# Three edits to the first third of a hybrid encoder layer: rotary tables after the first norm, gate stores on ScalarE's queue, half of the memory's values inside the scans

## The chip, the cores and the metric

The kernel runs on one core of one Trainium2 chip. The core has five engines, each working through its own list of instructions in order: TensorE (PE) for matrix products, VectorE (DVE) and ScalarE (ACT) for elementwise work, GpSimd (POOL) for some elementwise work, and SyncE (SP), which here only starts transfers (DMAs). An engine that reaches an instruction whose input is not there stands until it is, and everything behind that instruction in its list stands with it. The metric is the device time of one execution in microseconds (us), lower is better.

## The reference, cut to what matters

One layer works on x (1024 tokens x 1024) and on a memory of 256 tokens:

```
h    = rms_norm(x) ; proj = h @ w_in            # q,k,v of attention, q,k,v of DeltaNet, gate, alpha, beta
attn = window_attention(rope(q), rope(k), v)    # 8 heads, 2 kv heads, +-128 tokens
dn   = gated_delta(conv(q,k,v), decay, beta)    # 4 heads, two directions, then * silu(gate)
x    = x + rms_norm([attn, dn] @ w_out)
x    = x + rms_norm(cross_attention(rms_norm(x), rms_norm(mem), w_cq, w_ckv, w_co))
out  = x + rms_norm(swiglu(rms_norm(x)))
```

Three pieces of this matter here. `rope` needs the sine and cosine of position x frequency for 1024 tokens (the rotary tables). The gate is silu(h @ w_gate), 512 columns, and is multiplied onto the DeltaNet's output. The cross-attention needs keys and values of the memory, mem @ w_ckv, each 256 x 1024. All products are taken in three parts of reduced-precision pieces (high x high, high x low, low x high), so each weight tile is cast (`whi`, on ACT) and its remainder taken (`wlo`, on DVE or POOL) before PE may use it.

## The kernel before

Stage 1 (about 0 to 200 us of the span) loads x in eight tiles of 128 tokens. Each tile is squared and summed (ACT, L230), its root inverted (ACT L168, DVE L169), scaled (DVE, L233, tile `xt`), transposed on PE (L239), and cast into a high part (ACT, L241, `hhi`) and a low part (DVE, L242, `hlo`). Two halves of four tiles each make `hT`. Then come the projections of the DeltaNet's q, k and v (PE, L276, weights by `load_w`, L103 to L125). Each projection is followed by a convolution: ACT copies it into `cp` (L298), DVE adds four shifted products (L301, `acc`, four instructions of 128x1024), ACT takes the silu (L302). `decays` (L486 to L493), `key_products`, `query_products` and `base_inverse` (L558 and L560: sixty small dependent DVE instructions for each pair of heads) follow in the order of `ORDER_1`.

The rotary tables (L398 to L415) belong to stage 1 in the text, behind the products for alpha and beta. For each half of the tokens, DVE issues eight instructions on `ang` (L405 to L411, with three of L410) and two on `sct` (L414, L415), and ACT two sines (L412, L413). They read `posi`, which a DMA on SP's queue loads (L400). The tables are first read in stage 2, by `attn_proj`.

Stage 2 (about 200 to 372 us) runs `ORDER_2`: A are the projections of the attention's q and k with the rotation, V its values, G the four gate projections, L the four `levels` that finish the inverses, W two attention windows each. `gate_proj` takes two banks of PSUM, writes silu of each into `gt` (ACT, L814), and stores it in `d_gate` in DRAM by a DMA on SP's queue (L815). `gt` shares the buffers "rop" (two) with the attention projections.

Stage 3 (about 372 to 520 us) runs `ORDER_3`: M is the memory's norm, each `s01` one step of the two groups' scans over the eight chunks (the ninth flushes), W two windows, K one of eight blocks of the memory's keys (24 products of 128x256 on PE, remainder on POOL), V one of two halves of its values (48 products of 128x512, in four weight chunks of 512 KB, remainder on DVE, L104). A tail of windows and values, until about 559 us, leads to the first product with `w_out` (`mid_gemm`, L1102, tile `pmg`). The weights `wraw`, `whi` and `wlo` are rings of two buffers each, used by everything that calls `load_w`, and PSUM is one pool of five banks (`pc`) in stage 3, which must be empty before `mid_gemm` gets its banks.

What sets the order on each engine is a list scheduler that runs when the kernel is built: it places instructions by its own model of time, by order in the text, and by `high_priority` for weight loads; `tc.issue_after(x)` adds that an instruction comes behind x. So a change of three lines can move any instruction of these stages. Within the first `mid_gemm` the lists of before and after come together again.

The semaphores that DMAs count on are eight, DMAHW0 to DMAHW7, taken in turn by all DMAs of the schedule; a DMA waits until the DMA eight places ahead of it, which had the same one, is done.

Of the kernel before, what the change touches and what calls it, by code (L numbers as in the profile page):

```python
# [19 lines left out]
P = 128  # L20
# [4 lines left out]
HALF = 512  # L25
# [10 lines left out]

ORDER_1 = ("k0 k1 E0 K0 U0 E1 K1 U1 S0 q0 v0 q1 C0 v1 E2 C1 k2 E3 k3 q2 K2 U2 v2 K3 U3 S1 q3 C2 v3 C3 B0 B1").split()
ORDER_2 = "L0 L1 A4 V A0 A1 G0 G1 L2 L3 W W W A2 A3 G2 G3 W".split()
ORDER_3 = ("M " + "s01 W K " * 5 + "s01 K " * 3 + "s01 V V").split()


_NAMES = ["ident", "mUi", "mLi", "m5", "m6", "band0", "band1", "band2", "mU", "mL", "ones"]
# [34 lines left out]
def tile_hybrid_block(  # L77
# [6 lines left out]
    nc = tc.nc  # L84
    x, mem, out = x[0], mem[0], out[0]
    w_in, w_out, w_cq, w_ckv, w_co = w_in[0], w_out[0], w_cq[0], w_ckv[0], w_co[0]
# [7 lines left out]
    def f32(ap):  # L94
        return ap.bitcast(F32)
# [4 lines left out]
    def split(hi, lo, src, scale=None, eng=None):  # L100

        if scale is None:
            nc.scalar.copy(hi, src)  # L103
            return (eng or nc.vector).tensor_tensor(lo, src, f32(hi), ALU.subtract)  # L104
        nc.scalar.activation(hi, src, AF.Identity, scale=scale)
        return nc.vector.scalar_tensor_tensor(lo, src, scale, f32(hi), ALU.mult, ALU.subtract)
# [68 lines left out]
    def gain(n, k):  # L175
        return cols[:, gain_at[n] + k:gain_at[n] + k + 1]
# [7 lines left out]
    d_gate = dram.tile([512, S], F32, name="d_gate")  # L184
# [38 lines left out]
    for hf in range(2):  # L223
# [12 lines left out]
        for k in range(KT):  # L236
# [5 lines left out]
            cut = nc.vector.scalar_tensor_tensor(lo[:, k, :], pt, g, f32(hi[:, k, :]), ALU.mult, ALU.subtract)  # L242
# [36 lines left out]
    def proj(src_cols, eng=None):  # L279
        whi, wlo = load_w(src_cols, KT, P, eng)  # L280
        pp = [pg.tile([P, 512], F32, tag="pg", name="pg") for _ in range(2)]
        gemm_b(whi, wlo, hT, pp)
        return pp
# [36 lines left out]
    t1 = pa1.enter_context(pool("t1b", 1, side="right"))  # L320

    wab = t1.tile([P, KT, 16], F32, tag="wab", name="wab", bufs=1)
    nc.sync.dma_start(wab, w_in[:, 2816:2832].rearrange("(k p) n -> p k n", p=P))
    wabr = tb.tile([P, KT, P], F32R, tag="V", name="wabr", bufs=1)
    with tc.issue_after(scaled.ins):
        nc.vector.tensor_scalar(wabr, hT[0][0].bitcast(F32)[:, :, 0:P], 0.0, None, ALU.mult)
# [70 lines left out]
    sct = ra.tile([P, 2, S], F32, tag="sct", name="sct")  # L397
    sinT, cosT = sct[:, 0], sct[:, 1]  # L398
    posi = wt.tile([P, S], I32, tag="inv1", name="posi")
    nc.sync.dma_start(posi, positions[0].partition_broadcast(P))  # L400
    for hf in range(2):
        sl = slice(hf * HALF, (hf + 1) * HALF)
        work = wt.tile([P, 2, HALF], F32, tag="inv0", name="ang")
        ang, rn = work[:, 0], work[:, 1]
        nc.vector.tensor_copy(ang, posi[:, sl])  # L405
        nc.vector.tensor_scalar(ang, ang, rope_f, None, ALU.mult)
        nc.vector.tensor_scalar(rn, ang, 1.0 / (2.0 * math.pi), MAGIC, ALU.mult, ALU.add)
        nc.vector.tensor_scalar(rn, rn, MAGIC, None, ALU.subtract)
        for cc in (c1, c2, c3):
            nc.vector.scalar_tensor_tensor(ang, rn, -cc, ang, ALU.mult, ALU.add)  # L410
        nc.vector.tensor_scalar(ang, ang, math.pi, -math.pi, ALU.min, ALU.max)  # L411
        nc.scalar.activation(sinT[:, sl], ang, AF.Sin, scale=rope_s)  # L412
        nc.scalar.activation(cosT[:, sl], ang, AF.Sin, scale=0.5)  # L413
        nc.vector.tensor_tensor(cosT[:, sl], cosT[:, sl], cosT[:, sl], ALU.mult)  # L414
        nc.vector.tensor_scalar(cosT[:, sl], cosT[:, sl], -2.0, 1.0, ALU.mult, ALU.add)  # L415
# [342 lines left out]
    def issue(order, table):  # L758
        for o in order:
            table[o[0]](*(int(c) for c in o[1:]))  # L760
# [48 lines left out]
    def gate_proj(h):  # L809

        pp = proj(w_in[:, 2304 + h * P:2304 + (h + 1) * P])
        for hf in range(2):
            gt = trp.tile([P, HALF], F32, tag="rop", name="gt")
            nc.scalar.activation(gt, pp[hf], AF.Silu)  # L814
            nc.sync.dma_start(d_gate[h * P:(h + 1) * P, hf * HALF:(hf + 1) * HALF], gt)  # L815

    issue(ORDER_2, {"A": attn_proj, "V": value_proj, "G": gate_proj, "L": levels, "W": next_windows})
    dump("d_q", d_q); dump("d_k", d_k); dump("d_gate", d_gate)
    p1.close()
# [186 lines left out]
    def scan_step(pairs):  # L1006

        for _ in range(4):
            for s_ in pairs:
                next(s_, None)  # L1010

    issue(ORDER_3, {"s": lambda *gs: scan_step([scans[g] for g in gs]), "W": next_windows, "M": memory_norm,
                    "K": next_keys, "V": next_values})
# [452 lines left out]
    for k in range(KT):  # L1466
        pt = turned_k(first_rows, k, (PG, PN, PX, PG)[k // 2])
        cut = split(x1h[:, k, :], x1l[:, k, :], pt, gain("ffn", k))
# [406 lines left out]
```

## Time and profile before

| what | value |
|---|---|
| median of 3 runs | 1534.7 us (1529.84 to 1535.23) |
| the profiled execution | 1540.26 us, span 1538.0 us |
| mean granted clock of TensorE | 0.989 |
| PE busy | 1481.9 us (96% of the span) |
| DVE busy | 1095.6 us (71%) |
| ACT busy | 787.4 us (51%) |
| POOL busy | 364.7 us (24%) |

The profile is of one execution. "Busy" is the time in which an engine executes; the rest is idle, and the profile names what ended each idle stretch (the releaser). PEclk is the share of TensorE's full clock that was granted in a stretch: at 0.5 a product takes twice as long, and PE is busy for it all the same, so a stage loses time in two ways, by PE's idle time and by a low clock. A row of the timeline reads: start in us, duration, engine, line, operation, output<-inputs, shapes, count, and in brackets the idle time before it and what ended that. SPq is the queue on which SP starts DMAs.

### The profile page before, as it was taken

The page shows a single profiled execution, that of the slowest core. Times are in us where ns is not written, and L with a number is a line of the kernel's source. Part 1 is how long each engine was busy: PE and PEld are TensorE (multiplying, and loading weights), DVE is VectorE, ACT ScalarE, POOL GpSimd, SP SyncE. Part 2 cuts the span into 40 slices and gives each one's busy share as a digit, 9 for nine tenths or more (in the row PEclk, how much of TensorE's full clock was granted, in tenths as well). Part 3 has the DMA queues.
Part 4 walks back from the last instruction along what each step waited for, and adds up shares of the span by engine and source line. Part 5 has one row for each costly group of instructions (what it writes and reads, how often), then busy time and mean ns, then how long its engine had stood idle before and what let it go on. Part 6 is the DMA issues. An engine that isn't in the chain of part 4 may idle for free.

```text
span 1538.0 us, 21325 instructions
## 1 busy us (share of the span) xinstructions
PE 1481.9 (96%) x7437; PEld 1245.3 (81%) x7437; DVE 1095.6 (71%) x1801; ACT 787.4 (51%) x1608; POOL 364.7 (24%) x394
## 2 busy tenths in 40 slices
PE   6999999998899989999999999999999999999998
PEld 5888888787899768888788867888888888888787
DVE  6768998366798856447657768776868774696566
ACT  7578844567548755455545685323232232454533
POOL 0011133331237202152300101433434332000020
PEclk9999999999999989999999999999999999999999
DMA  6235464455998655357733743433435333853355
GB/s 200 68 103 152 118 187 136 143 171 141 318 306 253 223 187 194 111 195 255 248 121 134 229 165 118 129 123 124 132 108 171 124 99 108 311 210 101 110 176 166
DMA packets 257751, 256.34 MB, mean 167 GB/s; under 512 B 18128, under 2 KB 190317, under 8 KB 257645
## 3 DMA queue, kind: packets, MB, share of 16 engines
q1 hardware_dynamic: 257645, 255.00, 51.8%
q8 instruction: 58, 0.95, 0.3%
q14 instruction: 48, 0.39, 0.1%
HBM read 178.63 MB, written 73.70 MB: 164 GB/s over the span
## 4 chain that ended last, share of the span: by engine, by line
PE 70%; DVE 10%; DMA 8%; ACT 6%; issue 4%; SPq 2%; POOL 0%; DVEq 0%; ACTq 0%; POOLq 0%
PE pg L276 9%; PE pE L1512 8%; PE pD L1512 8%; PE pA L1512 6%; PE pmg L1102 6%; PE pdX L1718 5%; PE pst L1318 5%; PE pB L1512 4%; PE pcq L276 3%; PE pdA L1718 2%; PE psc L841 2%; PE pdD L1718 2%; DMA wpart<-in_w_co_dram 1%; DMA b<-in_w_down_dram 1%; PE pco L1217 1%
## 5 line engine op out<-in xcount | busy, mean ns | idle before, releaser
L103 ACT CAST whi<-wraw 128x1024 fp32r<-128x1024 f32 x96 | 100.9, 1052 | 131.4 <-DMA wraw<-in_w_gate_up_dram 35.7
L276 PE MATMUL pg<-hlo,whi 128*128 128x512 f32 x352 | 141.3, 401 | 0.0
L276 PE MATMUL pg<-hhi,whi 128*128 128x512 f32 x352 | 140.9, 401 | 0.1
L276 PE MATMUL pg<-hhi,wlo 128*128 128x512 f32 x352 | 140.5, 399 | 0.0
L104 POOL TENSOR_TENSOR wlo<-wraw,whi 128x1024 fp32r<-128x1024 f32 x36 | 87.4, 2429 | 179.3 <-ACT whi L103 179.3
L1512 PE MATMUL pA<-b,whi 128*128 128x512 f32 x352 | 110.7, 396 | 3.6 <-ACT m L1539 2.8
L104 DVE TENSOR_TENSOR wlo<-wraw,whi 128x1024 fp32r<-128x1024 f32 x60 | 73.2, 1221 | 49.7 <-ACT whi L103 41.6
L1512 PEld LDWEIGHTS pA<-b,whi 128*128 128x128 f32 x352 | 65.7, 189 | 19.0 <-ACT m L1539 4.0
L276 PEld LDWEIGHTS pg<-hhi,whi 128*128 128x128 f32 x352 | 67.4, 191 | 14.0 <-ACT hhi L241 0.7
L276 PEld LDWEIGHTS pg<-hlo,whi 128*128 128x128 f32 x352 | 67.3, 191 | 13.0
L276 PEld LDWEIGHTS pg<-hhi,wlo 128*128 128x128 f32 x352 | 67.5, 192 | 12.7
L1718 PE MATMUL pdX<-dhl,whi 128*128 128x512 f32 x264 | 76.1, 390 | 1.7 <-DVE zv L1777 0.8
L1595 POOL TENSOR_TENSOR act<-act,up 128x512 f32<-128x512 f32 x33 | 50.8, 1538 | 83.2 <-DVE up L1594 61.8
L103 ACT CAST whi<-araw 128x1024 fp32r<-128x1024 f32 (+1 forms) x36 | 35.3, 981 | 68.4 <-PE pdX L1718 27.6
L1512 PE MATMUL pA<-b,wlo 128*128 128x512 f32 x176 | 69.4, 395 | 0.5 <-DVE wlo L104 0.5
L104 DVE TENSOR_TENSOR wlo<-araw,whi 128x1024 fp32r<-128x1024 f32 (+1 forms) x36 | 40.8, 1133 | 36.8 <-ACT whi L103 36.7
L1567 POOL TENSOR_TENSOR sr<-wraw 128x512 f32<-128x512 f32 x22 | 30.7, 1397 | 151.4 <-DMA wraw<-in_w_gate_up_dram 102.1
L301 DVE SCALAR_TENSOR_TENSOR acc<-cp,cols,acc 128x1024 f32<-128x1024 f32 x48 | 61.9, 1298 | 0.2
L1718 PEld LDWEIGHTS pdX<-dhl,whi 128*128 128x128 f32 x264 | 49.3, 188 | 13.0 <-issue 1.1
L103 ACT CAST dhl<-b 128x512 fp32r<-128x512 f32 x66 | 40.3, 620 | 31.0 <-PE pdA L1718 13.2
L1512 PE MATMUL pB<-s0h,s1h 128*128 128x512 f32 x176 | 54.7, 392 | 1.2 <-ACT s1h L103 1.2
L103 ACT CAST s0h<-sr 128x512 fp32r<-128x512 f32 x22 | 13.7, 622 | 80.7 <-POOL sr L1567 80.2
(503 smaller groups left out, 4314.4 us busy)
## 6 DMA issues: line engine op xcount, KB each, us to landing
wraw<-in_w_gate_up_dram SPq DMA_DIRECT2D x54, 512.0 KB, 3.8
kv<-d_kv SPq DMA_DIRECT2D x32, 512.0 KB, 7.0
wraw<-in_w_in_dram SPq DMA_DIRECT2D x22, 512.0 KB, 3.7
b<-in_w_down_dram SPq DMA_DIRECT2D x20, 512.0 KB, 6.6
araw<-d_as SPq DMA_DIRECT2D x20, 512.0 KB, 3.7
pz<-d_pz SPq DMA_DIRECT2D x32, 256.0 KB, 7.1
wraw<-in_w_ckv_dram SPq DMA_DIRECT2D x16, 512.0 KB, 6.7
wraw<-in_w_out_dram SPq DMA_DIRECT2D x16, 512.0 KB, 3.8
```

The costliest lines, as they stand in the source:

```text
L103: nc.scalar.copy(hi, src)
L104: return (eng or nc.vector).tensor_tensor(lo, src, f32(hi), ALU.subtract)
L276: nc.tensor.matmul(p_, w[:, k, :], ah[a][:, k, :], start=(k == 0 and i == 0), stop=(k == nk - 1 and i == 2))
L301: nc.vector.scalar_tensor_tensor(acc, cp[:, t:t + S], taps[t], acc, ALU.mult, ALU.add)
L841: nc.tensor.matmul(out[:, d, h, :], lt[:, d, h, :], rt[:, d, h, :], start=True, stop=True)
L1102: nc.tensor.matmul(pp[t], act[a][:, k, tt], w_[:, kk, :], start=(k == 0 and i == 0), stop=(k == KT - 1 and i == 2))
L1217: nc.tensor.matmul(po, vr_[a][:, kt, cs], pts[kt][b_], start=(kt == 0 and i == 0), stop=(kt == 1 and i == 2))
L1318: nc.tensor.matmul(bank, a[:, tt], w, start=(start and i == 0), stop=(stop and i == 2), skip_group_check=not check)
L1512: nc.tensor.matmul(out_, w[a][:, k, :], xx[b_][:, k, :], start=(start and k == 0 and i == 0), stop=(k == HK - 1 and i == 2), skip_group_ch ...
L1567: nc.gpsimd.tensor_tensor(s[0], b_[:, 0:HK], b_[:, HK:], ALU.add)
L1595: nc.gpsimd.tensor_tensor(o_, o_, up, ALU.mult)
L1718: nc.tensor.matmul(banks[t], a[:, k - k0, tt], w, start=(first and k == 0 and i == 0), stop=(k == NB - 1 and i == 2), skip_group_check=not ...
```

## The change

Rotary tables: the DMA of `posi` is placed behind that of `wab` (the weights of alpha and beta) on SP's queue, and the first instruction on `ang` of each half behind `cut`, the last `hlo` of the first norm. Gate stores: the same eight DMAs are started by ScalarE. Values: `ORDER_3` had its fifth to eighth key blocks in a row and both V at the end; now one V stands behind the sixth scan step, and the last K behind the ninth.

```diff
-ORDER_3 = ("M " + "s01 W K " * 5 + "s01 K " * 3 + "s01 V V").split()
+ORDER_3 = ("M " + "s01 W K " * 5 + "s01 V " + "s01 K " * 2 + "s01 K V").split()
...
-    nc.sync.dma_start(wab, w_in[:, 2816:2832].rearrange("(k p) n -> p k n", p=P))
+    wab_load = nc.sync.dma_start(wab, w_in[:, 2816:2832].rearrange("(k p) n -> p k n", p=P))
...
-    nc.sync.dma_start(posi, positions[0].partition_broadcast(P))
+    with tc.issue_after(wab_load.ins):
+        nc.sync.dma_start(posi, positions[0].partition_broadcast(P))
...
-        nc.vector.tensor_copy(ang, posi[:, sl])
+        with tc.issue_after(cut.ins):
+            nc.vector.tensor_copy(ang, posi[:, sl])
...
-            nc.sync.dma_start(d_gate[h * P:(h + 1) * P, hf * HALF:(hf + 1) * HALF], gt)
+            nc.scalar.dma_start(d_gate[h * P:(h + 1) * P, hf * HALF:(hf + 1) * HALF], gt)
```

The changed file has two lines more from L401 on, so L814 before is L816 after, and so on (L405 is L407, L301 stays).

The first place is VectorE's list while the second half of x is normed. Before:

```order
L405 CAST ang<-posi 128x512
L169 RECIPROCAL rs<-rs 128x1
L406 TENSOR_SCALAR ang<-ang,CE 128x512
L233 TENSOR_SCALAR xt<-xt,rs 128x1024
L169 RECIPROCAL rs<-rs 128x1
L269 TENSOR_SCALAR nega<-nega 128x8
L407 TENSOR_SCALAR ang<-ang 128x512
L233 TENSOR_SCALAR xt<-xt,rs 128x1024
```

After, at the same place and on to the first convolution:

```order
L169 RECIPROCAL rs<-rs 128x1
L233 TENSOR_SCALAR xt<-xt,rs 128x1024
L169 RECIPROCAL rs<-rs 128x1
L269 TENSOR_SCALAR nega<-nega 128x8
L233 TENSOR_SCALAR xt<-xt,rs 128x1024
L261 CAST mU_r<-CE 128x128
L262 CAST mL_r<-CE 128x128
L326 TENSOR_SCALAR wabr<-hhi_152 128x1024
L242 SCALAR_TENSOR_TENSOR hlo_239<-ps,gcol,hhi_238 128x512 x8
L327 CAST wabr<-wab 128x8x16
L328 TENSOR_TENSOR wabr<-wab,wabr 128x8x16
L407 CAST ang<-posi 128x512
```

No instruction on `ang` stands ahead of the last two `xt` and the eight `hlo` any more; the twenty instructions of the tables stand between those of the first convolutions and of alpha and beta.

The second place is ScalarE's list at the end of stage 2, with the waits that each instruction carries. Before:

```order
L692 ACTIVATE sc,ssum<-sc,nm 128x384 x3
L814 ACT_TABLE_LOAD [waits DMAHW3_49]
L814 ACTIVATE gt<-pg 128x512 [waits PE_49]
L696 ACT_TABLE_LOAD
L696 ACTIVATE es<-es 128x4 [waits Pool_49]
L956 ACTIVATE mjk,mss<-mt 128x1024
L956 ACTIVATE mjk,mss<-mt 128x1024 [waits DMAHW5_49,Activation_49]
L103 CAST ph<-ptw 128x512 [waits PE_49]
L103 CAST ph<-ptw 128x512 [waits DVE_49,PE_49]
L814 ACT_TABLE_LOAD [waits DMAHW4_49]
L814 ACTIVATE gt<-pg 128x512 [waits PE_49]
```

After:

```order
L816 ACT_TABLE_LOAD [waits DMAHW2_49]
L816 ACTIVATE gt<-pg 128x512 [waits PE_49]
L817 DMA d_gate<-gt 128x512 [waits DMAHW5_49,Activation_49]
L958 ACTIVATE mjk,mss<-mt 128x1024
L958 ACTIVATE mjk,mss<-mt 128x1024 [waits Activation_49]
L103 CAST ph<-ptw 128x512 [waits DVE_49,PE_49]
L816 ACTIVATE gt<-pg 128x512 [waits DMAHW4_49,PE_49]
L817 DMA d_gate<-gt 128x512 [waits DMAHW7_49,Activation_49]
```

Two loads of activation tables are gone there (over the whole list 34 stand where 36 stood: L814's four became three, and L696's four became three), and the two stores now stand in ScalarE's list, each with a wait on a DMA semaphore. Six of the eight stores carry such a wait.

The third place is PE's list where the first half of the values begins. Before, it begins behind the last transposes of the scans' flush (L933, `psc<-ident,ol`):

```order
L709 MATMUL ptw<-ident,sc 128x128 x4
L714 MATMUL pow<-ph,vhl 128x512
L933 MATMUL psc<-ident,ol 128x128 x4
L997 MATMUL pcv<-whi,mT_4077 128x512
L997 MATMUL pcv<-whi,mT_4078 128x512
L997 MATMUL pcv<-wlo,mT_4077 128x512
```

After, it begins between steps of the scans (L843, `psc`, are the scans' products), some 230 products earlier in the list, and 24 key products (`pck`) and the second half follow the flush:

```order
L685 MATMUL psw<-khi,qs 128x384
L685 MATMUL psw<-klo,qs 128x384
L935 MATMUL psc<-ident,ol 128x128 x4
L999 MATMUL pcv<-whi,mT_4077 128x512
L999 MATMUL pcv<-whi,mT_4078 128x512
L999 MATMUL pcv<-wlo,mT_4077 128x512
```

So 48 of the 96 value products left the stretch between the flush and the first `pmg`, and 24 key products came to it. The number of instructions on PE, DVE and POOL is unchanged; ScalarE has eight DMAs more and two table loads fewer, SP eight DMAs fewer.

## The prediction

> **What bounds the kernel now.** I read the page first, then PE by stage, then what each idle stretch of PE waited for.
>
> ```profile
> span 1538.0 us, 21325 instructions
> ...
> PE 1481.9 (96%) x7437; PEld 1245.3 (81%) x7437; DVE 1095.6 (71%) x1801; ACT 787.4 (51%) x1608; POOL 364.7 (24%) x394
> ...
> PE 70%; DVE 10%; DMA 8%; ACT 6%; issue 4%; SPq 2%; POOL 0%; DVEq 0%; ACTq 0%; POOLq 0%
> ```
>
> PE is busy for 96% and makes 70% of the chain that ended last. The change takes no product away, so it can only win PE's idle time, 1538.0 - 1481.9 = 56 us, and what a low clock adds. It moves instructions in the first 560 us alone; there the stages read (columns: length, then busy time and count of PE, PEld, DVE, ACT, POOL, then PE's clock):
>
> ```profile
> 24.00:50.00 26.00, 22.16 (x101) 17.75 (x100) 18.16 (x39) 13.59 (x22) 0.00 (x0) 0.87 0.21 56
> 50.00:130.00 80.00, 80.00 (x403) 66.88 (x402) 60.78 (x80) 57.95 (x136) 8.29 (x22) 1.00 0.40 112
> 130.00:250.00 120.00, 117.22 (x623) 99.36 (x622) 110.18 (x201) 78.18 (x210) 25.31 (x50) 1.00 0.48 138
> 340.00:376.00 36.00, 32.42 (x181) 27.29 (x180) 18.18 (x47) 27.43 (x55) 8.05 (x16) 0.95 0.43 133
> 376.00:420.00 44.00, 39.30 (x294) 35.53 (x293) 34.66 (x93) 25.46 (x59) 9.23 (x8) 1.00 1.04 319
> 420.00:519.00 99.00, 94.84 (x759) 90.92 (x758) 88.77 (x236) 69.70 (x203) 52.47 (x62) 1.00 0.78 240
> 519.00:560.00 41.00, 34.43 (x153) 27.66 (x152) 27.67 (x57) 24.79 (x47) 2.17 (x2) 0.91 0.82 276
> ```
>
> Three stretches are open: the first norm (24 to 50), the end of stage 2 (340 to 376), and the tail behind the scans (519 to 560). From 50 to 130 PE never stops; from 130 to 250 DVE is at 110.18 / 120 = 92%, and in the scans at 88.77 / 99 = 90%, so there PE and DVE are near their limit together.
>
> **Term 1, the rotary tables.** In the first norm the chain is posi, ang, xt, transposes, hlo, products:
>
> ```profile
> 19.75 0.43 SPq L400 DMA_DIRECT2D posi<-in_positions_dram  x1
> 23.24 0.29 ACT L168 ACTIVATE rs<-ss,mhalf 128x1 f32<-128x1 f32 x1
> 27.19 0.43 DVE L405 CAST ang<-posi 128x512 f32<-128x512 int32 x1 [4.66 <-DMA posi<-in_positions_dram]
> 29.19 0.75 DVE L233 TENSOR_SCALAR xt<-xt,rs 128x1024 f32<-128x1024 f32 x1
> 31.18 2.14 DVE L410 SCALAR_TENSOR_TENSOR ang<-ang 128x512 f32<-128x512 f32 x3
> 34.49 1.11 PE L239 MATMUL ps<-ident,xt 128*128 128x128 f32 x4 [2.79 <-DVE hlo L242]
> ...
> 49.65 7.25 PE pg L334 x32
> ...
> 24.00:34.50 10.50, 6.66 (x39) 4.88 (x37) 7.17 (x18) 5.66 (x10) 0.00 (x0) 0.96 0.53 139
> 34.50:41.00 6.50, 6.50 (x23) 5.45 (x24) 5.92 (x11) 3.93 (x6) 0.00 (x0) 0.54 0.00 0
> ```
>
> The root that the last `xt` needs was there at 23.5 (second row), but DVE stood 4.66 us before `ang` for a transfer that has nothing to do with it, and scaled that `xt` only at 29.19. More `ang` work (2.14 us) stands ahead of `hlo`, PE runs dry for 2.79 us, and its clock falls to 0.54 for the 6.5 us that follow. Idle 10.50 - 6.66 = 3.8 us, slow clock 6.5 x 0.46 = 3.0 us: 6.8 us. After, nothing of the tables stands ahead of `xt` and `hlo`, so I take all 6.8 as won by the time the first projections end; the next limit is `hlo` itself, eight instructions that ACT feeds one by one.
>
> [...]
>
> The cost is that the tables' work is still to do:
>
> ```profile
> 24.00:50.00 26.00, 8.49 (x16) 2.48 (x4) 0.87 0.21 56
> 24.00:50.00 26.00, 2.22 (x4) 2.48 (x4) 0.87 0.21 56
> L301 DVE SCALAR_TENSOR_TENSOR acc<-cp,cols,acc 128x1024 f32<-128x1024 f32 x48 | 61.9, 1298 | 0.2
> ```
>
> The same window asked for `ang` alone (first row) and `sct` alone (second) gives DVE 8.49 + 2.22 = 10.7 us and ACT 2.48 us; the table load before the sines is merely at another place. All twenty DVE instructions now stand between the taps of the first convolutions (1298 ns each), ahead of the alpha and beta chain and of `decays`. DVE has 80 - 60.78 = 19.2 us idle from 50 to 130, so 10.7 us fit, but not all of that idle time can be moved into: DVE waits there for ACT and PE too. Ends: all 6.8 us kept; or DVE's list is the path and 10.7 - 6.8 = 3.9 us are lost. I take 4.5 won, nearer the upper end, because PE in that row is 80.00 of 80 on other projections; 2.3 us go where DVE runs at 92% (130 to 250). The moved `posi` DMA passes two weight loads and `wab`; those start 0.4 us earlier, and `ang` wants it ten us later than before: nothing.
>
> **Term 2, the gate stores.**
>
> ```profile
> SPq L815 <- ACT gt L814: 10.4, 4, 6.2
> SPq L815 <- ACT bs L632: 8.7, 2, 8.3
> L815 SPq DMA_DIRECT2D d_gate<-gt x8: 320/330/552, 270.7 to 372.6; - x8
> DMA to landing us min/median/max: 2.0/3.3/6.9
> PE ptm L966 <- ACT gt L814: 0.3, 1, 0.3
> ...
> 364.06 1.28 ACT L814 ACT_TABLE_LOAD   x1
> 365.97 1.28 ACT L696 ACT_TABLE_LOAD   x1
> 370.21 0.50 PE L714 MATMUL pow<-ph,vhl 128*128 128x512 f32 x1 [2.71 <-ACT ph L103]
> ...
> 373.00 0.87 SPq L856 DMA_DIRECT2D kv<-d_kv  x2
> ```
>
> SP stood 10.4 + 8.7 = 19.1 us before these stores. Queued behind them are `qr`, `pz`, `kv` and the key weights. No wait of PE from 40 to 376 names any of them, so the freed queue is worth little by itself; its share is the start of the scans, where `kv` and `kraw` come some 3 us earlier (they then wait for PE's last gate product instead) and PE idles 44 - 39.30 = 4.7 us. What PE did wait for at the end of stage 2 is ScalarE: 2.71 us for `ph`, behind the two table loads shown. Two loads less are 2 x 1.28 = 2.6 us; two stores in that place cost ScalarE their issue, which the trace shows on SP only, 0.87 / 2 = 0.43 us each (last row), 0.9 us. Queued behind each store on ScalarE are `ph` and the casts of the memory's norm, which PE waits for. A store that waits for its semaphore holds them up: at least nothing, at most a landing of 6.9 us. Ends: 5 us won (idle 3.6 us and clock 36 x 0.05 = 1.8 us of the stage) to 5 us lost (one full landing less 1.7 = 2.6 - 0.9). I take 2 won, near 2.6 - 0.9, since the transfers eight places ahead are older than a median landing of 3.3 us by then.
>
> [...]
>
> **Term 3, the values.**
>
> ```profile
> 459.25 1.79 PE pck L981 x15
> 552.95 1.09 PE L997 MATMUL pcv<-whi,mT 128*128 128x512 f32 x4
> 553.88 0.39 PE L997 MATMUL pcv<-wlo,mT 128*128 128x512 f32 x1
> 541.52 0.50 PE L714 MATMUL pow<-ph,vhl 128*128 128x512 f32 x1 [2.14 <-ACT ph L103]
> 559.29 0.80 PE L1102 MATMUL pmg<-whi,s0h 128*128 128x512 f32 x1 [2.55 <-ACT vv L1001]
> 541.00:549.00 8.00, 6.55 (x17) 5.20 (x18) 6.80 (x15) 3.50 (x6) 0.00 (x0) 0.58 0.75 251
> ```
>
> A value product takes 0.93 / 4 = 0.23 us, a key product 1.79 / 15 = 0.12. So 48 x 0.23 = 11.0 us leave the tail, 24 x 0.12 = 2.9 us come to it: 8.1 us of PE work go to the scans. There they cost the same 8.1 us unless they fill idle time: 4.7 + (99 - 94.84) = 8.9 us are idle in the two scan rows, but in pieces under 1 us. The gain must come from the tail: 41 - 34.43 = 6.6 us idle, and 41 x 0.09 = 3.7 us of slow clock. The tail's waits are on ScalarE's list (`ph` behind mraw's casts and `whi`) and on the last `vv`; with half the value chunks, half of 10.3, 5 us, should go. Against it: four remainders more on DVE, at the 1.22 us that `wlo` shows below, in scans where DVE is at 90%; I put 2 us there. Net 3 won. Ends: 8 won (all products fall into idle time) to 5 lost (DVE's 4 x 1.22 stretch the scans, the tail keeps its waits).
>
> ```profile
> L104 DVE TENSOR_TENSOR wlo<-wraw,whi 128x1024 fp32r<-128x1024 f32 x38 | 46.3, 1220 | 25.8 <-ACT whi L103 18.6 <-PE ps L490 4.0 <-DMA d_kv<-acc 2.1
> ```
>
> **Sum.** 4.5 + 2 + 3 = 9.5 us less. The profiled execution took 1540.26 us (span 1538.0 and 2.3 around it): 1530.8. It lies 5.6 us above the median of the runs shown, so on that median I expect 1534.7 - 9.5 = 1525 us.
>
> **The rivals.** (a) DVE takes back the whole lead: the tables between the taps delay `decays` and `base_inverse`, and where DVE is at 92% nothing is left of 6.8 us. For it speaks that row, against it 19.2 us of idle DVE just before. 1534.7 - 5 = 1530. (b) The scans grow by all of V: term 3 is 5 lost in place of 3 won, 1534.7 - 1.5 = 1533; for it speaks DVE's 90%, against it that the tail's waits are real. (c) The slow clock after the first norm has another cause and stays: 3 us less won, 1528. (d) Slower: ScalarE stands at its stores. Six of them wait for the transfer eight places ahead, most of which SP starts late or has just started; at a median landing of 3.3 us each that is 20 us of ScalarE, in a stretch where PE waits for it already. Were it all on the path, 1534.7 - 7.5 + 20 = 1547; it decides from 15 us on, for then the other two terms and 0.5% are eaten. Against it: ACT is at 27.43 / 36 there, and the older transfers have mostly landed. (e) The change does little at all, because the scheduler's new order puts small waits at other places in the 500 us that it shuffles: 1534.
>
> **How the numbers follow.** A measurement of this kernel tells about 0.5%, 7.7 us, from no change: faster is below 1527, slower above 1542. Chances: the forecast 0.52 (its own range 1516 to 1531), (a) 0.14, (b) 0.10, (c) 0.04, (d) 0.10, (e) 0.10. Of the forecast 0.44 lies below 1527 and 0.08 above; (a) to (c) mostly fall within 0.5% and give 0.05 below it; half of (e)'s misses are on the slow side. So faster 0.49, same 0.35, slower 0.16. The range takes in the bounds of terms 2 and 3 on the good side, 1513, and stops on the other between (b) and (d), 1540.
>
> **What would show it.** Right: no idle time of DVE before L407 near 27 us, PE busy from 24 to 41 at full clock, and the first `wabr` product near 43 in place of 49.7; SP without a wait on `gt`, and `kv` loaded before 373; the first `pmg` 8 to 11 us earlier. Wrong: PE waits on DVE in 60 to 250 that were not there; ScalarE idle before L817; steps of the scans longer by over a microsecond each; a clock below 1 between 420 and 519.

## The result, and the profile after

| | median | range | ratio to before |
|---|---|---|---|
| before | 1534.8 us (4 runs) | 1529.8 to 1535.2 | |
| changed | 1520.5 us (4 runs) | 1518.8 to 1523.5 | 0.9924 (0.9899 to 0.9950) |
| changed, in a second group of runs (e5), where before took 1535.6 us | 1522.4 us (6 runs) | 1520.2 to 1526.5 | 0.9910 (0.9890 to 0.9930) |

The change wins 12 to 14 us by these ratios; their intervals reach from 8 to 17. One run of before, 1845 us long at a mean clock of 0.754, is left out of every mean below. The page of the profile after, and the same stretches that the prediction showed of before (columns: length, then busy time and count of PE, PEld, DVE, ACT, POOL, then the clock):

```profile
span 1516.8 us, 21323 instructions
...
PE 1471.5 (97%) x7437; PEld 1239.2 (82%) x7437; DVE 1101.3 (73%) x1801; ACT 784.2 (52%) x1606; POOL 362.8 (24%) x394
```

```profile
24.00:50.00 26.00, 26.00 (x133) 21.72 (x132) 19.14 (x29) 15.80 (x24) 0.13 (x2) 1.00 0.37 101
50.00:130.00 80.00, 80.00 (x404) 67.11 (x404) 61.16 (x90) 58.83 (x140) 7.37 (x21) 1.00 0.39 110
130.00:250.00 120.00, 117.19 (x621) 99.10 (x620) 112.41 (x206) 76.05 (x204) 27.48 (x50) 1.00 0.49 139
340.00:376.00 36.00, 32.39 (x198) 28.71 (x196) 24.52 (x63) 28.90 (x60) 7.11 (x9) 0.95 0.66 170
420.00:519.00 99.00, 96.45 (x709) 90.42 (x710) 83.90 (x219) 66.37 (x191) 44.07 (x57) 0.98 0.70 221
519.00:560.00 41.00, 37.95 (x181) 30.65 (x180) 30.37 (x49) 27.84 (x46) 0.40 (x2) 0.96 0.89 298
```

From 24 to 130 PE no longer stops and its clock is full. These rows compare equal times, though, and the changed kernel is further on at each of them. A fairer cut is at points of the program: the first `wabr` product (the end of the first norm), the first scan product `psc` on `kv` and `pz`, the first `pmg`, and the end. Before, before profiled a second time (experiment e9), and after, in this order:

```profile
0.00:49.50 49.50, 37.49 (x163) 29.49 (x164) 31.33 (x61) 32.53 (x57) 0.69 (x13) 0.93 0.49 156
49.50:375.50 326.00, 316.50 (x1664) 267.67 (x1663) 244.29 (x451) 209.37 (x504) 76.17 (x158) 0.98 0.48 137
375.50:559.30 183.80, 168.38 (x1204) 154.01 (x1202) 150.69 (x384) 119.75 (x307) 63.87 (x72) 0.98 0.86 268
```

```profile
0.00:48.40 48.40, 36.21 (x162) 28.31 (x163) 30.91 (x61) 32.04 (x57) 0.69 (x13) 0.96 0.51 159
48.40:372.70 324.30, 314.42 (x1664) 266.17 (x1663) 244.96 (x452) 209.24 (x504) 76.74 (x158) 0.99 0.48 138
372.70:555.80 183.10, 167.87 (x1203) 154.21 (x1201) 150.74 (x384) 119.68 (x307) 63.86 (x72) 0.98 0.86 269
```

```profile
0.00:43.20 43.20, 34.75 (x162) 28.07 (x163) 26.54 (x48) 30.05 (x54) 0.69 (x13) 1.00 0.61 190
43.20:361.30 318.10, 312.15 (x1670) 264.64 (x1670) 254.47 (x471) 209.26 (x505) 75.42 (x158) 1.00 0.48 138
361.30:543.90 182.60, 170.22 (x1211) 156.44 (x1210) 152.19 (x383) 120.18 (x307) 63.15 (x72) 0.97 0.85 267
```

Length less PE's busy time is PE's idle time. Before: 12.0, 9.5 and 15.4 us, 36.9 in all; before again: 12.2, 9.9 and 15.2, 37.3; after: 8.5, 6.0 and 12.4, 26.8. So in these profiles the change takes 10 us of idle time away: 3.5 in the first norm, 3.5 from there to the scans, 3.0 behind. Some 5 us of the norm's are a wait for the constants at the very start (4.90 us before, 5.62 after). Between the two executions of before the clock differs more than the idle time: 0.93 against 0.96 in the first row.

How well does idle time come back when the same kernel runs again? The three rows together agree within 0.4 us for before and within 1.3 us for the changed kernel (25.5 in e5); a single row differs by up to 1.1. Behind the first `pmg` it scatters more: the last 4200 products stand in the same order in every kernel here, and PE's idle time among them is 16.4 to 20.1 us in the fourteen profiles. The runs without a profile have a span and a clock. PE's busy time less its slow clock, span x (1 - clock), is 1462 to 1466 us in all fourteen profiles, so span x clock less 1465 is an estimate of a run's whole idle time, good to some 2 us. By it before was idle for 48 to 60 us, 53.6 in the mean of its runs, and the changed kernel for 43 to 52, 45.5 in the mean of its ten. So of some 13 us, 8 are idle time and 5 are clock.

### The profile page after: what moved, and what is told of

Same layout as the page of the kernel before. It is cut to its first block, busy times and chain, and to the rows that moved or that the text cites. A ratio compares the mean times of both kernels' runs of the same rounds, so it can differ in the third digit from the quotient of the medians.

```text
span 1516.8 us, 21323 instructions
## 1 busy us (share of the span) xinstructions
PE 1471.5 (97%) x7437; PEld 1239.2 (82%) x7437; DVE 1101.3 (73%) x1801; ACT 784.2 (52%) x1606; POOL 362.8 (24%) x394
## 4 chain that ended last, share of the span: by engine, by line
PE 64%; DVE 8%; DMA 5%; ACT 2%; issue 2%; POOL 1%; SPq 0%; DVEq 0%; ACTq 0%; POOLq 0%
PE pE L1514 8%; PE pD L1514 8%; PE pA L1514 6%; PE pmg L1104 6%; PE pdX L1720 6%; PE pst L1320 5%; PE pdA L1720 4%; PE pB L1514 4%; PE pcq L276 3%; PE psc L843 2%; PE pdD L1720 2%; DMA wpart<-in_w_co_dram 1%; PE pg L276 1%; DMA kv<-d_kv 1%; PE pcv L999 1%
## 5 line engine op out<-in xcount | busy, mean ns | idle before, releaser
L276 PEld LDWEIGHTS pg<-hhi,whi 128*128 128x128 f32 x352 | 66.5, 189 | 13.4 <-ACT hhi L241 0.3
L276 PEld LDWEIGHTS pg<-hlo,whi 128*128 128x128 f32 x352 | 66.5, 189 | 12.5
L276 PEld LDWEIGHTS pg<-hhi,wlo 128*128 128x128 f32 x352 | 66.5, 189 | 12.5
L301 DVE SCALAR_TENSOR_TENSOR acc<-cp,cols,acc 128x1024 f32<-128x1024 f32 x48 | 63.0, 1314 | 0.2
L1720 PEld LDWEIGHTS pdX<-dhl,whi 128*128 128x128 f32 x264 | 49.3, 188 | 12.7 <-ACT dhl L103 1.1
L103 ACT CAST dhl<-b 128x512 fp32r<-128x512 f32 x66 | 40.4, 620 | 31.9 <-PE pdA L1720 13.6
```

The costliest lines, as they stand in the source:

```text
L276: nc.tensor.matmul(p_, w[:, k, :], ah[a][:, k, :], start=(k == 0 and i == 0), stop=(k == nk - 1 and i == 2))
L301: nc.vector.scalar_tensor_tensor(acc, cp[:, t:t + S], taps[t], acc, ALU.mult, ALU.add)
L1720: nc.tensor.matmul(banks[t], a[:, k - k0, tt], w, start=(first and k == 0 and i == 0), stop=(k == NB - 1 and i == 2), skip_group_check=not ...
```

## The experiments

With three edits there are eight kernels. All were run, and beside them four others. In the table, idle time is cut as above and comes from one profiled execution; "slow clock" is the mean over a kernel's runs of span x (1 - clock), and for before it was 14.8, 14.6 and 13.8 us in the three groups of runs. "All idle" is the estimate above, of the whole span, in the mean of a kernel's runs. "Change" is (ratio - 1) x 1535 us.

| kernel | ratio (95%) | change | idle: norm | to the scans | scans and tail | slow clock | all idle |
|---|---|---|---|---|---|---|---|
| before, and again (e9) | 1 | 0 | 12.0, 12.2 | 9.5, 9.9 | 15.4, 15.2 | 14.4 | 53.6 |
| e1: rotary | 0.9944 (0.9926 to 0.9961) | -8.6 | 9.1 | 5.5 | 15.0 | 9.2 | 50.7 |
| e2: gate | 0.9964 (0.9951 to 0.9977) | -5.5 | 12.4 | 9.2 | 11.4 | 12.4 | 50.7 |
| e3: values | 0.9963 (0.9950 to 0.9977) | -5.7 | 12.4 | 9.1 | 11.3 | 10.6 | 52.5 |
| e6: rotary, gate | 0.9955 (0.9936 to 0.9975) | -6.9 | 8.8 | 5.8 | 18.4 | 10.0 | 51.8 |
| e7: gate, values | 1.0000 (0.9985 to 1.0015) | 0 | 12.7 | 8.8 | 13.6 | 15.0 | 53.9 |
| e4: rotary, values | 0.9920 (0.9901 to 0.9939) | -12.3 | 8.8 | 5.0 | 14.6 | 9.9 | 45.7 |
| e5: the whole change | 0.9910 (0.9890 to 0.9930) | -13.8 | 8.6 | 4.8 | 12.1 | 9.9 | 45.7 |
| e8: posi early | 0.9962 (0.9946 to 0.9979) | -5.8 | 11.6 | 7.8 | 11.9 | 12.7 | 51.0 |
| e10: gate stores by GpSimd | 0.9965 (0.9952 to 0.9979) | -5.4 | 13.6 | 7.9 | 12.6 | 12.5 | 49.8 |
| e11: whole, both values early | 0.9937 (0.9919 to 0.9956) | -9.7 | 9.1 | 6.1 | 11.8 | 12.7 | 45.2 |
| e12: e11 without gate | 0.9965 (0.9950 to 0.9979) | -5.4 | 9.2 | 5.2 | 12.1 | 13.4 | 48.2 |

### The edits one by one, and in pairs

e1 has the rotary lines of the diff alone, e2 its one gate line, e3 its `ORDER_3`; e4, e6 and e7 leave one of them out, e5 is the whole change.

```diff
 e1  +    with tc.issue_after(wab_load.ins):
     +        nc.sync.dma_start(posi, positions[0].partition_broadcast(P))
     +        with tc.issue_after(cut.ins):
     +            nc.vector.tensor_copy(ang, posi[:, sl])
 e2  +            nc.scalar.dma_start(d_gate[h * P:(h + 1) * P, hf * HALF:(hf + 1) * HALF], gt)
 e3  +ORDER_3 = ("M " + "s01 W K " * 5 + "s01 V " + "s01 K " * 2 + "s01 K V").split()
```

> The rotary edit alone (both lines); stores on SyncE, values at the end. Its list of ScalarE has 32 table loads, where before has 36 and the whole change 34. Sum of terms, as predicted: 4.5 us less than before (ends 6.8 less to 3.9 more), the first wabr product near 43, and the end of stage 2 as before but for that lead. Rival, one edit carries all: the lists that the rotary edit alone reshuffles hold most of what was gained, so 9 to 13 us less than before, with the first psc product 12 to 15 us earlier than the 375.5 of before, and no wait for ph of over 1.5 us at the end of stage 2.

> The gate stores on ScalarE alone. ScalarE's list keeps 36 table loads, as before. Sum of terms: 2 us less (ends 5 less to 5 more). Rival: term 2 rested on two table loads less, which this edit alone doesn't take away, so it is worth nothing: within 1.5 us of before, and the waits for ph at the end of stage 2 stay. Rival (d), ScalarE stands at its stores: 3 us or more slower, with PE waits behind it.

> The order of the values alone. Sum of terms: 3 us less (ends 8 less to 5 more): the stretch from the first psc to the first pmg, 375.5 to 559.3 = 183.8 us before, becomes about 181, with the wait for vv before pmg and the 2.1 us wait for ph gone. Rival (b): the scans grow by what the tail gives, 184 us or more, time unchanged.

> The whole change without the gate stores (rotary and values): 32 table loads. Sum of terms: 2 us slower than the whole change, which measured 14.3 us (0.9924) below before; so about 12 us below before. If the gate stores are worth nothing by themselves, or cost (two table loads more with them in this company): equal to the whole change or up to 3 us faster, 14 to 17 us below before.

> The whole change once more, beside the leave-one-out kernels on the same chip. Theory A, what the change wins is TensorE's idle time, and the rest of the difference is clock that comes and goes in steps of 1.7 us: its idle time up to the first pmg is again near 27 us (before 36.7), and its ratio is 0.990 to 0.993. Rival, the 26.8 us was a lucky execution: idle up to the first pmg of 29 us or more, and a ratio of 0.993 to 0.996.

> The whole change without the order of the values. Sum of terms: 3 us slower than the whole change. Theory A, rotary alone and gate alone won in different stages (6 to 7 us ahead of the first psc; 3.8 us behind it): both kept, idle up to the first pmg near 26 us, as fast as the whole change. Rival B, the gains behind the first psc come from whatever order the lists fall into, and don't add: idle behind the first psc 12 to 15 us, 1 to 3 us slower than the whole change.

> The whole change without the rotary edit. Sum of terms: 4.5 us slower than the whole change, 5 us under before. Theory A, gate and values are two separate gains: 8 us of idle time less behind the first psc (15.2 in before, 7 here), about 8 us and more under before. Rival B, they fill the same idle time: 11 to 12 us idle behind the first psc, as with either alone, 5 to 6 us under before. In both, the idle time of the first norm (12 us) and the 2.7 us wait for ph at the end of stage 2 are there.

**Rotary.** The idle time up to the scans, norm included, is 21.5 to 22.1 us in all six profiles without this edit (before twice, e2, e3, e7, e10), and 13.4 to 15.2 us in all seven that have it (e1, e4, e6, e11, e12, and the whole change twice). That is some 7 us, in whatever company: 3 to 4 in the norm, and as much again on the way to the scans. (e8, which moves the same tables' transfer alone, stands between, at 19.4.) Not all of the 7 us stay: in the mean of all runs e1 has 3 us less idle time than before in its whole span and e6 has 2, beside 4 to 5 us less of slow clock. Where the rest goes is not shown. What was won ahead of the scans can be read in the waits of PE from `wabr` to there (the largest; total, times, longest). In e2, without the rotary edit:

```profile
PE pow L714 <- ACT ph L103: 2.7, 1, 2.7
PE pow L714 <- DVE pl L104: 1.7, 2, 1.3
PE ps L630 <- DVE L L623: 1.6, 2, 1.2
PE ps L490 <- ACT gm L489: 1.6, 2, 0.9
```

In e1, with it:

```profile
PE ps L632 <- DVE mov L652: 1.3, 2, 1.1
PE ps L632 <- ACT mov L651: 1.0, 1, 1.0
PE pow L716 <- DVE pl L104: 1.0, 1, 1.0
```

The 2.7 us for `ph` at the end of stage 2 are there in every kernel whose ScalarE list has 36 table loads (before, e2, e3, e7, e8, e10), and in none that has 32 (e1, e4, e12) or 34 (e6, e11, the whole change). The waits for `gm` (of `decays`) go with it. So the two table loads that the prediction had put down to the gate stores belong to the rotary edit: it takes four away, and the stores bring two back. That the loads are the whole reason for the 2.7 us isn't shown, since the edit also moved the rest of ScalarE's list there.

**Gate and values.** In its profile each alone takes 4 us of idle time from the scans and the tail, and each is 5.5 us faster. Together they bring nothing (e7). The idle time that both win lies in the same place, behind the last scan product (`psc` on `vn`). From there to the first `pmg`, before and after:

```profile
508.90:559.30 50.40, 41.84 (x212) 34.39 (x210) 36.55 (x76) 32.98 (x73) 7.17 (x10) 0.93 0.73 244
```

```profile
506.20:543.90 37.70, 33.14 (x188) 27.18 (x187) 31.54 (x70) 26.22 (x68) 4.95 (x10) 0.95 0.77 261
```

This tail is idle for 8.6 us before (8.5 again in e9), 6.8 in e1 and 9.2 in e6. With the values moved it is 4.7 (e3), 5.2 (e7), 4.3 (e4), 4.6 and 4.0 (whole); with the gate stores alone it is 5.1 too. The waits from 515 us to the first `pmg` of before, and the same place with the whole change:

```profile
PE pow L714 <- ACT ph L103: 3.8, 3, 2.1
PE pmg L1102 <- ACT vv L1001: 2.6, 1, 2.6
PE psc L933 <- DVE ol L928: 1.3, 1, 1.3
PE pcv L997 <- ACT whi L103: 0.9, 1, 0.9
```

```profile
PE psw L685 <- DVE m L687: 2.5, 2, 1.5
PE pow L716 <- DVE pl L104: 1.3, 2, 0.8
PE ptw L711 <- DVE m L687: 0.3, 1, 0.3
PE pcv L999 <- DVE wlo L104: 0.2, 1, 0.2
```

The waits on ScalarE (`ph`, `vv`) are gone, and smaller ones on VectorE stand in their place. In the scans themselves the values filled no idle time: it was 6.9 us before and 7.8 with the whole change, while PE's busy time there went from 126.5 to 137.1.

Over the four pairs with and without it, an edit's mean effect is -7.6 us for rotary (-8.6, -1.4, -6.6, -13.8), +0.1 for gate (-5.5, +1.7, +5.7, -1.5) and -2.7 for values (-5.7, -3.7, +5.5, -6.9), each single difference to some 3 or 4 us. One number stays open. That gate and values win the same idle time says why they don't add, but not why e7 is no faster than before. Its profiled execution was the fastest of its twelve (span 1530.7, mean 1533.9); in the mean of all its runs idle time and slow clock are those of before (53.9 and 15.0 us). Where the gain of the tail goes there is not settled.

### posi early: the wait, or the work?

e8 starts the transfer of `posi` right behind the tiles of x, and leaves the tables' work among the norm's.

```diff
-    nc.sync.dma_start(posi, positions[0].partition_broadcast(P))
+    with tc.high_priority(1 << 30), tc.issue_after(xload[NT - 1].ins):
+        nc.sync.dma_start(posi, positions[0].partition_broadcast(P))
```

> Of before, one thing: posi's transfer is started right behind the eight tiles of x, so VectorE need not wait for it, while the instructions on ang stay among those of the norm, ahead of most hlo. Table loads 36, as in before. If the late transfer was what cost (4.66 us of VectorE): the norm's idle time falls from 12 to about 9 us, as in the rotary edit, and hlo begins 3 to 4 us earlier. If the instructions on ang ahead of hlo cost as much: TensorE still stands 2 us or more for hlo, idle 10.5 to 12 us. As for the whole time, if the 4 us that the rotary edit wins from 50 us on hang on the place of the tables' work (VectorE and ScalarE ahead of the scans), this kernel doesn't win them: 1.5 to 4 us under before against the 8.6 of the rotary edit.

VectorE no longer waits for the transfer (4.66 us in before, none listed here), and the norm's idle time hardly moves: 11.6 us where it was 12.0. What stands there now (e8's VectorE, then its ScalarE):

```profile
32.77 0.75 DVE L242 SCALAR_TENSOR_TENSOR hlo<-ps,gcol,hhi 128x512 fp32r<-128x512 f32 x1 [2.18 <-ACT hhi L241]
35.38 0.75 DVE L242 SCALAR_TENSOR_TENSOR hlo<-ps,gcol,hhi 128x512 fp32r<-128x512 f32 x1 [1.86 <-ACT hhi L241]
```

```profile
32.05 0.69 ACT L241 ACTIVATE hhi<-ps,gcol 128x512 fp32r<-128x512 f32 x1
32.76 1.28 ACT L413 ACT_TABLE_LOAD   x1
34.05 0.72 ACT L413 ACTIVATE sct<-ang,CE 128x512 f32<-128x512 f32 x1
34.68 0.67 ACT L241 ACTIVATE hhi<-ps,gcol 128x512 fp32r<-128x512 f32 x1
```

The first sine and its table load now stand between the first `hhi` of the second half and the next, and `hlo` waits for ScalarE instead of VectorE for `posi`. So what cost in the norm was the tables' work standing there, more than the late transfer. In the rotary edit the tables' place follows from the `posi` line alone: built with it and without the `cut` line, every list on all five engines is row for row as with both.

The kernel is 5.8 us faster all the same (3 to 8 by its interval; 1.5 to 4 were expected), with 3.5 us less idle time in the scans and the tail. Nothing of the edit is there, and no new order either: from 122 to 554 us of before, the traces of e8 and before have the same instructions in the same order on PE, VectorE, ScalarE and GpSimd. One difference is in when transfers land. In the scans of before PE waits 1.6 us for `kv` from DRAM, in e9 0.7, and for e8 no such wait is listed. What made the rest of the difference stays open.

### Gate stores by a third engine

```diff
-            nc.sync.dma_start(d_gate[h * P:(h + 1) * P, hf * HALF:(hf + 1) * HALF], gt)
+            nc.gpsimd.dma_start(d_gate[h * P:(h + 1) * P, hf * HALF:(hf + 1) * HALF], gt)
```

> Of before, the gate stores alone, started by GpSimd in place of SyncE; ScalarE has none, SyncE is as free as with the stores on ScalarE, and the table loads are 36. If a freed SyncE is what the gate stores alone won: 5 to 6 us under before, 11 to 12 us idle behind the first psc. If that gain was the order that the lists happened to fall into, it need not come again: anywhere from 5 us under to 5 us over before, and 2 us under if one has to say, with other waits behind the first psc than the stores on ScalarE left.

0.9965, the same as with the stores on ScalarE. That fits "a freed SyncE" by its time, but not by its place: what e10 and e2 win lies in the tail (4.9 and 5.1 us idle against 8.6), 130 us and more after the last gate store. There the lists of PE and VectorE are the same in both: e2 and e10 differ in the place of 13 products and of one VectorE instruction, all between 270 and 281 us, while e2 and before differ in that of some 265 products and 124 VectorE instructions, most of them from 360 us on. So the likeliest reason for this gain is the order that the scheduler falls into once SyncE has no stores; with the values or the rotary edit another order comes, without it. This is argued, not shown: e8 won 3.5 us in the same stages with the order unchanged. That a freed SyncE does nothing directly is not shown either, but no wait of PE speaks for it.

ScalarE stands at one of its eight stores (the changed kernel, the first and the last store; ACTq is ScalarE's queue):

```profile
256.92 0.59 ACT L816 ACTIVATE gt<-pg 128x512 f32<-128x512 f32 x1
261.35 0.37 ACTq L817 DMA_DIRECT2D d_gate<-gt  x1
267.74 0.62 ACT L676 CAST qs<-qr 128x512 fp32r<-128x512 f32 x1 [10.22 <-DMA qr<-d_q]
...
358.57 0.60 ACT L816 ACTIVATE gt<-pg 128x512 f32<-128x512 f32 x1 [1.14 <-PE pg L276]
359.19 0.33 ACTq L817 DMA_DIRECT2D d_gate<-gt  x1
```

Seven stores start 0.03 us behind the end of their `gt`, as the last one here. The first starts 3.8 us behind it (256.92 + 0.59 against 261.35), held by a semaphore: the store to `d_pz` that had last used the same one landed at 261.27. e5 has the same 3.8 us there, e6 4.0, e2 and e7 0.5 and 0.4. It costs nothing that the trace shows, for the input of ScalarE's next instruction comes only at 267.74. Starting a store takes 0.33 us, 2.6 for all eight, and of ScalarE's waits from 240 to 380 us only two, of 0.4 us each, are put down to `gt`.

### Twice the dose of values

e11 puts the second half of the values into the scans too; e12 is the same without the gate stores.

```diff
-ORDER_3 = ("M " + "s01 W K " * 5 + "s01 V " + "s01 K " * 2 + "s01 K V").split()
+ORDER_3 = ("M " + "s01 W K " * 5 + "s01 V " + "s01 K " + "s01 V " + "s01 K K").split()
```

> The whole change, with the second half of the values in the scans too (behind the eighth step) and the last two key blocks behind the flush. Dose of term 3: the stretch from the last vn product to the steady pmg products gets 8 us shorter again (40 to 32) and loses another 2 to 4 us of idle time, the scans grow by 8 us of products. If the scans take these products without new idle time: 2 to 4 us faster than the whole change. If VectorE, at 90% there, has become the limit: idle time in the scans goes from 8 to 11 us and more, and the kernel is as fast as the whole change or up to 3 us slower.

> The same without the gate stores on ScalarE. If the gate stores have no effect of their own, this is within 2 us of the run before it, and the same stretch behind the scans is as short. If the scans' idle time depends on the whole order, the two differ by 2 to 5 us in either direction.

Neither beats the whole change: e11 is 2 to 4 us behind it (the intervals meet), e12 further. The first `pmg` comes at 537.0 in place of 543.9, but then `mid_gemm` waits for its own weights and inputs (e11, waits of PE from 506 to 600):

```profile
PE pmg L1104 <- ACT s0h L103: 2.2, 1, 2.2
PE pmg L1104 <- ACT whi L103: 2.0, 1, 2.0
```

The scans' idle time did not grow (8.2 us, where the whole change has 7.8 and 8.1), so VectorE isn't the limit yet; the next work was not ready for an earlier end. No kernel here is faster than the changed one, and e4, which leaves the gate stores with SyncE, is as fast within the intervals.

### Before, a second time

> The kernel before, profiled a second time, to see what of the first profile is the execution and what the kernel. If clock and small waits come by chance: idle time ahead of wabr 12 to 13 us and from there to the first psc 9 to 10 us again, the 2.7 us wait for ph again; the 2.8 us wait for hlo again, with a slow clock behind it of 0, 3.4 or 6.8 us; slow stretches elsewhere at other places than 282, 542 and 559. If the clock follows from the list of instructions: slow at the same five places as before, 13.6 us of loss up to 600 us.

Idle time came back (37.3 against 36.9 us up to `pmg`), and the `ph` wait too. The clock was slow from 30, 282, 368, 538 and 555 us, where it had been slow from 33, 282, 371, 542 and 559. The second execution was ahead by 1 to 3.5 us at these points of the program, and four of the five stretches stand behind the same waits. The first does not. The 2.8 us wait for `hlo`, which was expected again, came as two, and the slow stretch (30.1 to 33.5) stands behind the other one:

```profile
30.17 1.33 PE L239 MATMUL ps<-ident,xt 128*128 128x128 f32 x5 [2.10 <-DVE xt L233]
35.81 0.66 PE L239 MATMUL ps<-ident,xt 128*128 128x128 f32 x4 [1.54 <-DVE hlo L242]
```

So the list says for the most part where the clock may fall; but two of the five stretches were half as long, and the loss up to the first `pmg` was 8.6 us in place of 12.0. Neither of the two readings had it whole.

## Why the prediction was right, point by point

**The sum.** 9.5 us less, 1525 us, were forecast; 12 to 14 less and 1520 to 1522 us came, inside the range and inside the likeliest case. The stages were right, two of the three prices were not (4.5, 2 and 3 us were counted; the mean effects above are 7.6, nothing and 2.7), and their errors partly cancelled. That the sum came so near is in part luck, the more so as e5's 13.8 us are 3.6 more than the mean effects add up to (10.2). The good end of the range, 1513, is 4 us below what the terms give on the median that the forecast uses (1534.7 - 4.5 - 5 - 8 = 1517).

**Term 1 (4.5 us) was too small, and its working failed at one step.** The chain posi, ang, `xt`, `hlo` was read rightly: `wabr` starts at 43.2, as forecast (near 43), and 3.5 us of idle time went where 3.8 were counted. The 3.0 us of slow clock were this one execution's: six profiled executions with that order of the norm lost 3.4, 1.7, 0, 1.7, 3.4 and 3.4 us there, 2.3 in the mean. The step that failed is "2.3 us go where DVE runs at 92% (130 to 250)". Nothing was given back: PE is busy for 80.00 of 80 us and 117.19 of 120 in the rows from 50 to 250, as before (117.22). VectorE had room for the work behind the norm, where 7.5 of the tables' 10.6 us stand between 50 and 65 us. And 3.5 to 5 us more were won between the norm and the scans, in the waits for `ph` and `gm` above all. Rival (a) is refuted by seven profiles.

**Term 2 (2 us) was wrong in its mechanism.** It rested on two table loads, and they go with the rotary edit; the `ph` wait it was to remove stands unchanged in e2. Its mean effect is nothing. No wait of PE names the stores, as it said; that the freed queue is worth little by itself fits this, but e2 and e10, each with that queue freed and 5.5 us faster, leave it unproven. The refusal of rival (d) was right: one stand of 3.8 us ahead of a later input, and 0.8 us of waits, not 20.

**Term 3 (3 us) was right in mechanism, and in size in the mean of pairs that lie from -6.9 to +5.5, so not without luck.** 8.1 us of products to the scans "unless they fill idle time": they filled none (6.9 us idle before, 7.8 after). The tail gave the gain: 4.0 to 4.6 us of idle time less, where half of 10.3 was expected with its clock. The 2 us kept back for VectorE were about right: of the four pairs, the scans' idle time rose by 2.1 us in two and changed by -0.3 and -1.2 to -1.5 in the others. Rival (b) is half true: the scans grow by all of V, and the change wins all the same.

**The clock.** The norm's gap of 2.79 us cost 3.4 us of clock in the profile of before, but it is not that dear every time: e2, with the same gap, lost none. Rival (c), which said the slow clock after the first norm has another cause, is wrong on the cause, for in all eight profiles with another order of the norm and without this gap (e8 and the seven with the rotary edit) the clock was 1.00 up to the first `wabr`, where five of the six with the order of before lost 1.7 or 3.4 us; it is right that the slow clock can't be counted in full.

**Rival (e)** had more in it than its 0.10: 3 to 4 us of idle time moved in tail and scans, far from the edits and in both directions (e2 and e10 down, e6 up). The new order of the lists is the likeliest reason there; in e8 as much moved with the order unchanged. The changed kernel got a good one, which the prediction did not foresee.

**The signs.** Those of being right came, and the first `pmg` was 15.4 us earlier than in the profile of before, where 8 to 11 were given. Some of being wrong came too: ScalarE stood ahead of the first L817; the clock from 420 to 519 was 0.98, for one slow step of 3.4 us behind a wait of 2.41 us for `kv`; and the scans are 11.5 us longer (133.4 to 144.9), over a microsecond a step, by the values in them.

## What to carry to other kernels

Before counting what a wait costs, take PE's idle time between points of the program, not at fixed times of the trace: it came back within some 1 us in a stage here, and shows in which stage an edit wins. Then set it beside the mean of many runs, for one profile can lie several us off. An edit's price can include stages it never touches, above all where a list scheduler sets the order, and two edits that each win 4 us may be winning the same 4 us: run them alone and in pairs, and read from the lists which edit really removed an instruction. Work that feeds nothing for 100 us, such as a table for a later stage, belongs behind the chain that PE waits for, and moving its transfer is not the same as moving its work.

## What the runs showed of the hardware

The slow clock came in steps. Where the clock was read through the span (before, after, e5 to e12), every slow stretch that was seen whole, but for the span's last microseconds, ran at 0.5 for about 3.4 or 6.8 us, and so cost 1.7 or 3.4 us. At 0.5, value products of before start 0.43 us apart (546.96 and 547.39 us), at full clock 0.23 (549.53 and 549.76). The same gap of 2.79 us before the same transposes led to two steps, one, or none. Before (shown in the prediction) lost two; e2's row of the gap and the stretch behind it, at full clock:

```profile
34.53 0.66 PE L239 MATMUL ps<-ident,xt 128*128 128x128 f32 x4 [2.79 <-DVE hlo L242]
...
34.50:41.00 6.50, 6.46 (x35) 5.42 (x36) 6.50 (x12) 5.28 (x9) 0.00 (x0) 1.00 0.00 0
```

e3's, with the clock at 0.57 over four microseconds:

```profile
35.80 0.66 PE L239 MATMUL ps<-ident,xt 128*128 128x128 f32 x4 [2.79 <-DVE hlo L242]
...
36.00:40.00 4.00, 4.00 (x17) 3.27 (x17) 4.00 (x8) 3.04 (x5) 0.00 (x0) 0.57 0.00 0
```

What decides between these, and what sets the length of a step, no run here shows. Over a whole execution the slow clock costs 8 to 15 us of 1520 in the mean of a kernel's runs: 14.4 us before, 8.4 and 9.9 after. About 5 of the 13 us that the change wins are clock. The number of gaps does not say why: from 17 us to the first `pmg` PE stood for 1 to 3 us 6 and 9 times in the two profiles of before, 8 and 6 times in the two of the changed kernel. Gaps of over 2 us were 4 and 3 there, against 1 and 1, and the clock lost 12.0 and 8.6 us, against 5.1 and 5.1. That fits, but four executions don't show it.
